# Where the modulation columns of a hybrid decoder layer are computed, and four output tiles written one by one

## The chip, the cores and the metric

The kernel runs on one core of one Trainium2 chip, in one launch. The metric is the device time of an execution in microseconds (us); the median of three runs stands for a kernel. About 0.2% is what a measurement of this kernel can tell from no change.

## The reference

One layer on x of 256 rows and 2048 columns, in f32, with three residual parts, each behind an RMSNorm that is shifted, scaled and gated by vectors computed from a conditioning row c:

```python
cond = jax.nn.silu(c)
mod = cond @ ada_w[l] + ada_b[l]                       # 9 vectors of 2048
sh1, sc1, gt1, sh2, sc2, gt2, sh3, sc3, gt3 = jnp.split(mod, N_MOD, axis=-1)
h = ada_in(x, norm_g[l, 0], sh1, sc1)                  # rmsnorm(x)*g*(1+sc) + sh
x = x + MACARON_W * gt1[:, None, :] * swiglu(h, ...)   # SwiGLU_1, inner width 5632
h = ada_in(x, norm_g[l, 1], sh2, sc2)
x = x + gt2[:, None, :] * hybrid_mixer(h, w_in[l], w_out[l], ...)   # 8 heads forgetting attention, 8 heads gated delta net
h = ada_in(x, norm_g[l, 2], sh3, sc3)
x = x + MACARON_W * gt3[:, None, :] * swiglu(h, ...)   # SwiGLU_2
...
return rmsnorm(x, final_norm)
```

## The kernel before, in words

**Layout.** x is held transposed: 16 tiles `x[:, j]` of 128 features by 256 rows. All weights are cut into 5392 tiles of 128 by 128 and laid out in DRAM in the order in which TensorE uses them, eight to a block, so there are 674 blocks of 512 KB. `Stream.next` hands out the next tile. At the first tile of a block it loads the block (`wraw`, on SP's queue), ScalarE rounds it to the high half `whi` (L127), and VectorE subtracts to get the low half `wlo` (L139). A product of f32 precision is made of three matmul terms: high by high, high weight by low activation, low weight by high activation. Raw, high and low halves have four buffers each, so a block's halves can be made up to three blocks ahead of TensorE.

**Stages by blocks.** SwiGLU_1 is done in two parts of its inner width. Blocks 0 to 111 are the gate and up products of its first 28 inner tiles (`gate_up_first`, matmuls L572 to L574 into `pgu`), 112 to 167 their down products, 168 to 263 the second part. The mixer's input projections are blocks 264 to 377, with the chains of the heads woven in; its output projection is blocks 378 to 409 (`po`, L492 and L493, two matmuls a tile). SwiGLU_2 takes the rest.

**The first stage** cannot have all of its input h at once, since h needs the modulation columns sc1 and sh1. The list `PIECES` cuts the contraction into pieces (group of eight inner tiles, first k, k from which a tile is finished on its own, end k). At the end of a piece the partial sums are moved out of PSUM: first copied by ScalarE, then added on VectorE (`acc`, L587), and with the last piece two adds (L590, L591), SiLU, a product (L523) and a split in halves (L506, L507) make the tile `hid`.

**The modulation columns.** The 9 vectors are 144 columns of 128 values. A column is one 1 MB load of 128 rows of `ada_w` (`adat`, on SP's queue) and one multiply-and-add-up on VectorE (L264) into `mod`. Two are made before the stream begins. The others are side work of the stream: at each block the rate of that block in `RATE` is added to a counter, and each time it reaches 1, `ada_col` issues the next column. The order is sc1 and sh1 by turns, then gt1, sh2, sc2, gt2, sh3, sc3, gt3. `ada_need` computes at once whatever is missing when a column is wanted; with both tables of rates every column has been issued by then. Inside the mixer (`W.late`) the VectorE part is put off by two blocks.

**Order of work.** The engines' programs are written out in program order by a scheduler that lets a later instruction go ahead only where the earlier one isn't ready in its own estimate of time; on the chip each engine then runs its list in that fixed order.

**The output projection.** The first four output tiles j = 0 to 3 are accumulated together in four PSUM banks, 64 weight tiles or 8 blocks, because the last head isn't ready at the start. Tiles 4 to 15 follow one by one, 16 weight tiles or 2 blocks each. The epilogue `after` of a tile does the gated residual (`residual`, L516 and L517), the square for the next norm (ScalarE, then GpSimd adds), and `norm2.y`, which scales the tile by 1 + sc3 for SwiGLU_2 (g at L389, high half on ScalarE L415, low half on VectorE L416). The epilogues of tiles 0 to 3 stand right behind the last of their products; the epilogue of each later tile stands in the next tile's products at i = `LATER` = 8 of 16.

Of the kernel before, what the change touches and what calls it, by code (L numbers as in the profile page):

```python
# [19 lines left out]
KD = D // P  # L20
# [12 lines left out]
GR = 24  # L33
NEG = -1e30

RATE = ((0, 0.5), (12, 0.45), (68, 0.06), (112, 0.5), (168, 0.38), (264, 0.0), (284, 0.26), (404, 0.0), (424, 0.125))
N_BIG, N_GDN = 3, 3
N_FIRST = 2
AHEAD = 4
# [2 lines left out]
HIDX = 3  # L42
MORE = True
LATER = 8
BEHIND = 2

HA = 128 + 16
# [45 lines left out]
class Stream:  # L93
# [36 lines left out]
    def next(self, mat, k, n, width=1):  # L130
        i = len(self.order)
        if i % WB == 0:
# [3 lines left out]
            self.l = lo.tile([P, WB * P], F32R, name="wlo")  # L136
            pace = [r_ for r_ in RATE if r_[0] <= b][-1][1]
            with self.behind():
                lo_ = nc.vector.tensor_tensor(self.l, r, self.h.bitcast(F32), ALU.subtract)  # L139
            with self.tc.issue_after(lo_.ins):  # L140
                self.settle(b - BEHIND)
            self.owed += 0.0 if self.quiet else pace
# [11 lines left out]
def layer_kernel(ctx: ExitStack, tc: tile.TileContext, xrow, c, adaw, cols, cst, w, out, order, dbg=None):  # L154
# [14 lines left out]
    def psb(name="psb"):  # L169
        return big.tile([P, 512], F32, name=name, tag="psb")  # L170

    def pss(name="pss"):
        return sml.tile([P, 512], F32, name=name, tag="pss")

    def psf(name="psf"):
        return sm2.tile([P, 512], F32, name=name, tag="psf")

    def psn(i, name):

        i %= 8  # L180
        return psb(name) if i < N_BIG else pss(name) if i < N_BIG + N_GDN else psf(name)
# [5 lines left out]
    x = keep.tile([P, KD, T], F32, name="x")  # L187
# [85 lines left out]
    def ada_need(m, j):  # L273

        while ada_st["i"] < ada_seq.index((m, j)) + 1:
            ada_col()
        W.settle()
# [23 lines left out]
    def sqrt_table(after):  # L301

        d = tiny.tile([P, 1], F32, name="dummy")
        return A.activation(d, after, AF.Sqrt, scale=0.0)

    def sumsq_add(j):

        if j == 0:
            sqa["acc"] = tmp.tile([P, T], F32, name="sqacc", bufs=1)
            A.activation(sqa["acc"], x[:, j], AF.Square)  # L310
            return
        s = tmp.tile([P, T], F32, name="sq")
        A.activation(s, x[:, j], AF.Square)
        if j == KD - 1:
            sqa["src"] = [sqa["acc"], s]
        else:
            G.tensor_tensor(sqa["acc"], sqa["acc"], s, ALU.add)
# [152 lines left out]
    def tick(us):  # L470
        clock["now"] += us
        for kind in chains:
            if chains[kind] and clock["now"] >= due[kind]:
                advance(kind)

    def finish(kind, h):

        while chains[kind] and chains[kind][0][0] <= h:
            advance(kind)
# [11 lines left out]
    def mm(ps, wt, act, first, last):  # L491
        PE.matmul(ps, wt[0], act.rearrange("p q (a b) -> p q b a", a=2), start=first, stop=False)  # L492
        PE.matmul(ps[:, :T], wt[1], woven(act[:, 0]), start=False, stop=last)  # L493
# [15 lines left out]
    def residual(ps, j, m_gt, half):  # L509
        ada_need(m_gt, j)  # L510
        g = mod[:, m_gt * KD + j : m_gt * KD + j + 1]
        if half:
            gh = tiny.tile([P, 1], F32, name="gh")
            V.tensor_scalar(gh, g, 0.5, None, ALU.mult)
            g = gh
        V.scalar_tensor_tensor(x[:, j], ps[:, :T], g, x[:, j], ALU.mult, ALU.add)  # L516
        i = V.scalar_tensor_tensor(x[:, j], ps[:, T:], g, x[:, j], ALU.mult, ALU.add)  # L517
        sqa["hold"] = i.ins
# [109 lines left out]
    def ffn(which, m_gt, early=None):  # L628
        fs = list(range(NF))
        with tc.tile_pool(name=f"hid{which}", bufs=PARTS[which][1] + HIDX) as hp, \  # L630
                tc.tile_pool(name=f"more{which}", bufs=1) as more:
            W.more = more if MORE else None
            for half in range(2):
# [7 lines left out]
                def after(j):  # L641
                    residual(pds.pop(j), j, m_gt, True)
                    if half == 1:
                        sumsq_add(j)
                        if which == 1:
                            if j < KD - 1:
                                A.activation(x[:, j], x[:, j], AF.Copy, scale=L("fng", j, 1))
                            else:
                                V.tensor_scalar(x[:, j], x[:, j], L("fng", j, 1), None, ALU.mult)
                        if j == KD - 4:  # L650
                            W.quiet = True
                        if j == KD // 2:
                            sqrt_table(x[:, j, :1])

                for j in range(KD):
                    ps = psb("pd")
                    for q, hd in enumerate(hids):
                        if j and q == LATER:
                            after(j - 1)
# [19 lines left out]
    for kind, i in (("x", 0), ("x", 1), ("c", 0), ("c", 1), ("x", 2), ("x", 3), ("c", 2), ("c", 3)):  # L679
        with nullcontext() if hold is None else tc.issue_after(hold):  # L680
            if kind == "c":
                hold = cond(i)
            else:
                t, q = divmod(i, 2)
# [64 lines left out]
    norm2 = Early(2, 6, 7)  # L749
# [5 lines left out]
    def mixer():  # L755
# [23 lines left out]
        def x_back(q):  # L779
            with tc.issue_after(W.last):  # L780
                nc.sync.dma_start(x[:, 4 * q : 4 * q + 4], xd[:, 4 * q : 4 * q + 4])
# [499 lines left out]
        owed = []  # L1281
        ko = [NH + h for h in range(4)] + list(range(6)) + [NH + h for h in range(4, NH)] + [6, 7]
        for js in [list(range(4))] + [[j] for j in range(4, KD)]:

            j = js[0]
            one_ = psf if j < 6 or j >= KD - 2 else pss if j < 8 else psb
            pj = [psn(i, "po") for i in range(len(js))] if len(js) > 1 else [one_("po")]
            if js[0] in BACK:
                x_back(1 + BACK.index(js[0]))
            for i, k in enumerate(ko):  # L1290
                for kind in ("gdn", "out") if k >= NH else ("fox",):
                    finish(kind, k % NH)
                if js[0] == 0 and i == KD - 1:
                    x_back(0)
                if owed and i == LATER:
                    owed.pop(0)()
                for q, j in enumerate(js):
                    mm(pj[q], W.next("o", k, j), oh_[k], i == 0, i == KD - 1)
                    tick(TILE_US)

            def after(js=js, pj=pj):
                for q, j in enumerate(js):
                    residual(pj[q], j, 5, False)
                    sumsq_add(j)
                    norm2.y(j)
                    if j == KD // 2:
                        sqrt_table(x[:, j, :1])

            if j == 3 or j == KD - 1:
                after()  # L1310
            else:
                owed.append(after)
        mx.close()

    if dbg is None or "mix" in dbg:
        mixer()
# [154 lines left out]
```

## Time and profile before

| | before |
|---|---|
| median of 3 runs | 1944.64 us (1944.19 to 1946.02) |
| profiled execution, its own time | 1944.91 us |
| its span, first to last instruction | 1943.1 us |
| TensorE (PE) matmul busy | 1903.0 us, 98% |
| VectorE (DVE) busy | 1555.1 us, 80% |
| ScalarE (ACT) busy | 1039.5 us, 53% |
| mean granted clock of TensorE | 0.993 |
| modulation columns on VectorE | 142, 334.6 us |
| low halves on VectorE | 674, 820.8 us |

The profile is one execution. A line of the timeline gives the start in us, the duration, the engine, the source line, the operation, its output and inputs, and in square brackets the idle time of the engine ahead of it and what ended that. A line of a list of waits gives who waited for whom, the total in us, how many times and the longest. A line of windows gives busy time and number of instructions of each engine in that stretch, the clock granted to TensorE (1.00 is full), and the share and rate of the DMA engines. A line of groups gives number, busy time and mean duration in ns. Busy times of successive instructions overlap a little, because an instruction starts before the one ahead has drained.

### The profile page before, as it was taken

Reading aid. Unit: us, or ns where it says so; the run is one execution under the profiler, and the core shown is the slowest. Engines: PE = TensorE matmul, PEld = TensorE weight load, DVE = VectorE, ACT = ScalarE, POOL = GpSimd, SP = SyncE. Lnnn points to the kernel's source line nnn. Section 1 sums busy time; section 2 is a strip of 40 time slices with the busy share of each in tenths; the row PEclk is TensorE's granted clock in tenths of the full one; section 3 lists DMA queues with packets and bytes.
Section 4 is the critical chain, followed back from the end, with each engine's and each line's share of the span. In section 5 each row is a group of like instructions: output and inputs, shape, how many; then the busy total and the mean of one; then the engine's idle time right before and its main releaser. Section 6 shows DMA issues by size and latency. Waiting matters only on the chain.

```text
span 1943.1 us, 33703 instructions
## 1 busy us (share of the span) xinstructions
PE 1903.0 (98%) x13086; PEld 1774.5 (91%) x13087; DVE 1555.1 (80%) x2414; ACT 1039.5 (53%) x1647; POOL 57.4 (3%) x55
## 2 busy tenths in 40 slices
PE   8999999999999999999999999999999999999998
PEld 7999999988999988889989998999999999999997
DVE  6999888989999997789987989877676765666654
ACT  7433555433455446857757655665554445555553
POOL 0000000000000020000000002100000000000011
PEclk9999999999999999999999999999999999999999
DMA  9998867999989985596567567677777766666663
GB/s 374 350 344 345 294 215 265 400 374 376 361 347 348 349 307 211 197 330 219 204 254 250 207 229 281 206 246 264 240 246 262 244 231 199 203 199 202 200 201 120
DMA packets 129490, 519.58 MB, mean 267 GB/s; under 512 B 18217, under 2 KB 21545, under 8 KB 111153
## 3 DMA queue, kind: packets, MB, share of 16 engines
q1 hardware_dynamic: 129330, 517.42, 74.1%
q8 instruction: 103, 1.69, 0.3%
q14 instruction: 57, 0.47, 0.1%
HBM read 512.89 MB, written 4.47 MB: 266 GB/s over the span
## 4 chain that ended last, share of the span: by engine, by line
PE 77%; DVE 12%; issue 4%; ACT 3%; DMA 2%; SPq 0%; DVEq 0%; ACTq 0%
PE pd L492 12%; PE pu L488 10%; PE pg L488 10%; PE pd L493 6%; PE pu L489 5%; PE pg L489 5%; DVE wlo L139 5%; PE pgu L574 4%; PE pgu L572 4%; PE pgu L573 4%; DVE adat L264 3%; PE po L492 2%; PE pp L795 2%; PE pp L796 2%; PE pp L797 2%
## 5 line engine op out<-in xcount | busy, mean ns | idle before, releaser
L139 DVE TENSOR_TENSOR wlo<-wraw,whi 128x1024 fp32r<-128x1024 f32 x674 | 820.8, 1225 | 263.8 <-ACT whi L127 262.6
L127 ACT CAST whi<-wraw 128x1024 fp32r<-128x1024 f32 x674 | 698.3, 1045 | 509.4 <-PE pd L492 178.1
L492 PE MATMUL pd<-hid,whi 128*128 128x512 f32 x1408 | 462.1, 382 | 0.0
L493 PE MATMUL pd<-hid,wlo 128*128 128x256 f32 x1408 | 384.8, 274 | 2.7 <-DVE wlo L139 2.7
L264 DVE CUSTOM_DVE_ANT_0 adat<-adat,cs,colt 128x2048 f32<-128x2048 f32 x142 | 334.6, 2357 | 7.6 <-DMA adat<-in_ada_dram 7.4
L488 PE MATMUL pg<-hs,whi 128*128 128x512 f32 x912 | 302.1, 382 | 0.5 <-DVE shc L439 0.5
L488 PE MATMUL pu<-hs,whi 128*128 128x512 f32 x912 | 302.2, 382 | 0.0
L492 PEld LDWEIGHTS pd<-hid,whi 128*128 128x128 f32 x1408 | 266.0, 189 | 36.7 <-DVE hid L507 0.2
L493 PEld LDWEIGHTS pd<-hid,wlo 128*128 128x128 f32 x1408 | 270.2, 192 | 6.0 <-DVE wlo L139 5.6
L489 PE MATMUL pu<-hs,wlo 128*128 128x256 f32 x912 | 249.3, 273 | 0.0
L574 PE MATMUL pgu<-hs,wlo 128*128 128x256 f32 x896 | 240.7, 278 | 8.3 <-DVE wlo L139 8.0
L489 PE MATMUL pg<-hs,wlo 128*128 128x256 f32 x912 | 248.8, 273 | 0.0
L572 PE MATMUL pgu<-hs,whi 128*128 128x256 f32 x896 | 244.8, 276 | 0.8 <-DVE acc L587 0.5
L573 PE MATMUL pgu<-hs,whi 128*128 128x256 f32 x896 | 244.5, 276 | 0.0
L488 PEld LDWEIGHTS pg<-hs,whi 128*128 128x128 f32 x912 | 172.4, 189 | 24.9 <-ACT shc L438 0.7
L488 PEld LDWEIGHTS pu<-hs,whi 128*128 128x128 f32 x912 | 172.4, 189 | 23.6
L795 PE MATMUL pp<-hs,whi 128*128 128x256 f32 x656 | 188.4, 288 | 1.1 <-ACT hs L379 1.1
L797 PE MATMUL pp<-hs,wlo 128*128 128x256 f32 x656 | 182.2, 278 | 0.0
L796 PE MATMUL pp<-hs,whi 128*128 128x256 f32 x656 | 181.9, 277 | 0.0
L574 PEld LDWEIGHTS pgu<-hs,wlo 128*128 128x128 f32 x896 | 168.8, 193 | 11.0 <-DVE wlo L139 10.8
L489 PEld LDWEIGHTS pu<-hs,wlo 128*128 128x128 f32 x912 | 175.0, 192 | 1.4 <-DVE wlo L139 1.4
L489 PEld LDWEIGHTS pg<-hs,wlo 128*128 128x128 f32 x912 | 175.1, 192 | 0.3
(335 smaller groups left out, 2585.9 us busy)
## 6 DMA issues: line engine op xcount, KB each, us to landing
wraw<-in_w_dram SPq DMA_DIRECT2D x674, 512.0 KB, 4.4
adat<-in_ada_dram SPq DMA_DIRECT2D x142, 1024.0 KB, 7.5
xr<-in_xr_dram SPq DMA_DIRECT2D x4, 512.0 KB, 5.6
adaf<-in_ada_dram SPq DMA_DIRECT2D x4, 512.0 KB, 8.5
xd<-x SPq DMA_DIRECT2D x4, 512.0 KB, 6.9
rw<-rowd SPq DMA_DIRECT2D x16, 128.0 KB, 4.2
x<-xd SPq DMA_DIRECT2D x4, 512.0 KB, 5.6
out_dram<-o SPq DMA_DIRECT2D x8, 256.0 KB, 2.6
```

The costliest lines, as they stand in the source:

```text
L127: self.cast = self.nc.scalar.copy(self.h, r).ins
L139: lo_ = nc.vector.tensor_tensor(self.l, r, self.h.bitcast(F32), ALU.subtract)
L264: V.tensor_tensor_reduce(t, t, cs, 1.0, L("adab", q, 1), ALU.mult, ALU.add, mod[:, q : q + 1])
L488: PE.matmul(ps, wt[0], both, start=(k == 0), stop=False)
L489: PE.matmul(ps[:, T:], wt[1], part(k, HI), start=False, stop=(k == KD - 1))
L492: PE.matmul(ps, wt[0], act.rearrange("p q (a b) -> p q b a", a=2), start=first, stop=False)
L493: PE.matmul(ps[:, :T], wt[1], woven(act[:, 0]), start=False, stop=last)
L572: PE.matmul(o, wh, part(k, HI), start=first and s == 0, stop=False, skip_group_check=skip)
L573: PE.matmul(o, wh, part(k, LO), start=False, stop=False, skip_group_check=skip)
L574: PE.matmul(o, wl, part(k, HI), start=False, stop=last, skip_group_check=skip)
L795: PE.matmul(pp[i][:, :T], wh, hh, start=(k == 0), stop=False)
L797: PE.matmul(pp[i][:, :T], wl, hh, start=False, stop=(k == KD - 1))
```

## The change

Three things change. The table of rates gets new stretches in SwiGLU_1: blocks 28 to 32 and 49 to 55 have a rate of 0.25, the others up to 65 have 0.5, and blocks 66 to 111 have 0.2 instead of 0.45 and 0.06. The mixer's input projections have 0.255 up to block 375, and from there to 423 the rate is 0, which takes in the output projection; from 424 it is 0.16. The epilogues of the first four output tiles no longer stand together behind their products: each goes on the list `owed`, as those of the later tiles do, and as long as that list has more than one, two of them are taken per output tile, at i = 3 and i = 11; else one at i = 8. Whatever is left is done at the end.

```diff
-RATE = ((0, 0.5), (12, 0.45), (68, 0.06), (112, 0.5), (168, 0.38), (264, 0.0), (284, 0.26), (404, 0.0), (424, 0.125))
+RATE = ((0, 0.5), (28, 0.25), (33, 0.5), (49, 0.25), (56, 0.5), (66, 0.2), (112, 0.5), (168, 0.38), (264, 0.0), (284, 0.255), (376, 0.0), (424, 0.16))
...
 LATER = 8
+SLOTS = (3, 11)
...
             one_ = psf if j < 6 or j >= KD - 2 else pss if j < 8 else psb
+            slots = SLOTS if len(owed) > 1 else (LATER,)
...
-                if owed and i == LATER:
+                if owed and i in slots:
                     owed.pop(0)()
...
-            def after(js=js, pj=pj):
-                for q, j in enumerate(js):
-                    residual(pj[q], j, 5, False)
-                    sumsq_add(j)
-                    norm2.y(j)
-                    if j == KD // 2:
-                        sqrt_table(x[:, j, :1])
-
-            if j == 3 or j == KD - 1:
-                after()
-            else:
-                owed.append(after)
+            def after(j, ps):
+                residual(ps, j, 5, False)
+                sumsq_add(j)
+                norm2.y(j)
+                if j == KD // 2:
+                    sqrt_table(x[:, j, :1])
+
+            owed += [lambda j=j, ps=ps: after(j, ps) for j, ps in zip(js, pj)]
+        while owed:
+            owed.pop(0)()
         mx.close()
```

## The prediction

> **What bounds the kernel now.** I read the page first, then the list of waits of TensorE, then the windows of 5 us around each wait, then VectorE's timeline inside those windows. The share of busy time of TensorE leaves 40 us of the span.
>
> ```profile
> span 1943.1 us, 33703 instructions
> PE 1903.0 (98%) x13086; PEld 1774.5 (91%) x13087; DVE 1555.1 (80%) x2414; ACT 1039.5 (53%) x1647; POOL 57.4 (3%) x55
> ```
>
> So a gain has to come out of single waits of TensorE, or out of stretches in which its clock was low. The waits that this change can reach are these; wlo is the low half of a block of eight weight tiles, which VectorE makes by one subtraction, in program order with everything else that it does.
>
> ```profile
> PE pgu L574 <- DVE wlo L139: 8.0, 10, 2.3
> PE po L493 <- DVE wlo L139: 2.0, 1, 2.0
> PE po L492 <- ACT whi L127: 0.7, 1, 0.7
> PE pgu L572 <- DVE acc L587: 0.5, 2, 0.3
> ```
>
> pgu is the first gate/up stage of SwiGLU_1, po the output projection. TensorE's steady rate there is read from two undisturbed windows (PE, PEld, DVE, ACT, POOL busy with counts, then clock, DMA share, GB/s): 450 matmuls at 3 a tile in 50 us are 2.67 us for a block of 8 tiles; 1223 at 2 a tile in 200 us are 2.62 us.
>
> ```profile
> 250.00:300.00 50.00, 50.00 (x450) 50.00 (x450) 38.35 (x56) 25.45 (x36) 0.00 (x0) 1.00 0.72 234
> 1300.00:1500.00 200.00, 200.00 (x1223) 183.69 (x1222) 142.13 (x175) 99.72 (x143) 0.00 (x0) 1.00 0.74 251
> ```
>
> **The output projection.** It runs from block 378 to 409. The windows that hold wlo alone count the blocks (busy us of VectorE, number, clock, DMA share, GB/s):
>
> ```profile
> 0.00:1168.10 1168.10, 470.98 (x389) 0.99 0.80 298
> ...
> 0.00:166.90 166.90, 60.00 (x50) 0.99 0.92 355
> ```
>
> Blocks count from 0, so the subtraction at 1168.02 belongs to block 388 and the next one, at 1178.32, to block 389; in the same way 166.98 is block 50. Between them VectorE does the epilogues of the first four output tiles in one go, and one modulation column (adat):
>
> ```profile
> 1168.02 1.23 DVE L139 TENSOR_TENSOR wlo<-wraw,whi 128x1024 fp32r<-128x1024 f32 x1 [2.70 <-ACT whi L127]
> 1169.17 0.87 DVE L516 SCALAR_TENSOR_TENSOR x<-po,mod,x 128x256 f32<-128x256 f32 x2
> ...
> 1173.80 2.40 DVE L264 CUSTOM_DVE_ANT_0 adat<-adat,cs,colt 128x2048 f32<-128x2048 f32 x1
> ...
> 1178.32 1.21 DVE L139 TENSOR_TENSOR wlo<-wraw,whi 128x1024 fp32r<-128x1024 f32 x1
> ```
>
> ```profile
> 1175.81 0.60 PE L492 MATMUL po<-oh,whi 128*128 128x512 f32 x2
> ```
>
> TensorE runs out of low halves at about 1176.1 and waits, and the two slices from 1175 us show the rest of the bill: 11 and 22 matmuls where an undisturbed slice of 5 us has 33 (before it), and a clock of 0.68 after the wait.
>
> ```profile
> 1165.00:1170.00 5.00, 5.00 (x33) 4.64 (x32) 2.30 (x5) 1.48 (x2) 0.00 (x0) 1.00 1.01 390
> ...
> 1175.00:1180.00 5.00, 2.30 (x11) 1.53 (x11) 5.00 (x9) 2.04 (x3) 2.58 (x2) 0.98 0.01 4
> 1180.00:1185.00 5.00, 5.00 (x22) 4.39 (x22) 5.00 (x7) 1.89 (x3) 1.06 (x1) 0.68 0.89 340
> ```
>
> 33 matmuls short are 5.0 us. The waits alone are 2.7, and the clock costs 5 x 0.32 + 5 x 0.02 = 1.7, together 4.4. I take the middle, 4.7 us, as the price of this place.
>
> What the change does here. The epilogues now stand in the order at slots 3 and 11 of the following tiles, so only three of them (slot 3 and 11 of tile 4, slot 3 of tile 5) come before wlo 389, and no column. Prices of VectorE's work in this stage:
>
> ```profile
> L139 DVE TENSOR_TENSOR wlo<-wraw,whi 128x1024 fp32r<-128x1024 f32 x31 | 38.2, 1236 | 5.0 <-ACT whi L127 5.0
> L264 DVE CUSTOM_DVE_ANT_0 adat<-adat,cs,colt 128x2048 f32<-128x2048 f32 x7 | 16.5, 2350 | 0.0
> L416 DVE SCALAR_TENSOR_TENSOR hs<-x,g,hs 128x256 fp32r<-128x256 f32 x15 | 13.5, 904 | 0.2 <-ACT hs L415 0.2
> L517 DVE SCALAR_TENSOR_TENSOR x<-po,mod,x 128x256 f32<-128x256 f32 x15 | 7.1, 486 | 0.1
> L516 DVE SCALAR_TENSOR_TENSOR x<-po,mod,x 128x256 f32<-128x256 f32 x15 | 7.0, 476 | 0.0
> L389 DVE SCALAR_TENSOR_TENSOR g<-mod,colt 128x1 f32<-128x1 f32 (+1 forms) x15 | 2.3, 160 | 0.1
> ```
>
> By durations an epilogue is 0.476 + 0.486 + 0.904 + 0.160 = 2.03 us. Successive instructions overlap a little: from 1169.17 to 1178.32 are 9.15 us, less one column of 2.35 leaves 6.8 for four epilogues, 1.70 each. Three of them end at 1169.17 + 5.1 = 1174.3, wlo 389 is done at 1175.5, and TensorE needs it when block 388 ends, about 1176.1. The wait goes. What is late next is the run of tiles 4 to 6, each with two epilogues: 2 x 1.70 + 2 x 1.13 = 5.67 us of VectorE against 2 x 2.62 = 5.23 of TensorE, three times 0.44 = 1.3 us, of which the margin at block 389 pays 0.6. That is a stall of up to 0.7; if epilogues don't overlap (2.03 and 1.24), three times 1.3 less 0.6 is 3.3. I take 0.5, because the 1.70 was measured in this place. So the projection gains 4.7 - 0.5 = 4.2 us, bounds 1.4 and 5.0. The other six columns that leave lie beside a TensorE that doesn't wait; taking 2.35 us each from a free VectorE earns nothing. ScalarE's two operations per tile only move with their tile. On SP's queue seven loads of a column go with them:
>
> ```profile
> adat<-in_ada_dram SPq DMA_DIRECT2D x142, 1024.0 KB, 7.5
> ```
>
> No weight block that TensorE waits for here was held up by one (its wait was for wlo, and the DMA stood at 0.01 during it), so their leaving earns nothing, and they join stages counted below.
>
> **The columns of SwiGLU_1.** A running sum of the rates gives the block at which each column is issued. Up to block 27 there are 13 before and 14 after; in 28 to 32 two against one; in 33 to 48 seven against eight; in 49 to 55 three against two; at block 65 both have 30. From 66 to 111 three become nine. The waits lie where eight partial sums are added in a burst (acc), with a column in it:
>
> ```profile
> 72.64 0.38 PE L574 MATMUL pgu<-hs,wlo 128*128 128x256 f32 x1 [0.58 <-DVE wlo L139]
> ...
> 105.62 0.38 PE L574 MATMUL pgu<-hs,wlo 128*128 128x256 f32 x1 [2.25 <-DVE wlo L139]
> 119.04 0.38 PE L574 MATMUL pgu<-hs,wlo 128*128 128x256 f32 x1 [0.43 <-DVE wlo L139]
> ...
> 168.25 0.38 PE L574 MATMUL pgu<-hs,wlo 128*128 128x256 f32 x1 [2.25 <-DVE wlo L139]
> ```
>
> Counted by wlo, these are blocks 17, 28, 33 and 50. With the waits for acc the first place costs 0.58 + 0.5 = 1.1.
>
> Block 50. Before, VectorE idles 2.19 us ahead of the burst and then has a column inside it:
>
> ```profile
> 157.31 0.69 DVE L587 TENSOR_TENSOR acc<-pgu,acc 128x512 f32<-128x512 f32 x1 [2.19 <-PE pgu L574]
> ...
> 162.91 2.34 DVE L264 CUSTOM_DVE_ANT_0 adat<-adat,cs,colt 128x2048 f32<-128x2048 f32 x1
> ```
>
> After, the columns are those of blocks 48 and 51: the first fits the idle 2.19, the second comes behind wlo 50. That makes wlo 50 2.34 us earlier against a wait of 2.25: gain 2.25, nothing if column 48 is put into the burst. Behind this wait the clock also fell, worth 5 x 0.05 + 5 x 0.29 = 1.7; behind the equal wait at 105.62 it did not:
>
> ```profile
> 105.00:110.00 5.00, 4.38 (x39) 4.38 (x40) 5.00 (x6) 1.05 (x1) 0.00 (x0) 1.00 0.71 222
> ...
> 165.00:170.00 5.00, 2.75 (x22) 2.55 (x22) 5.00 (x8) 1.05 (x1) 0.00 (x0) 0.95 0.80 293
> 170.00:175.00 5.00, 5.00 (x34) 5.00 (x33) 5.00 (x7) 1.67 (x3) 0.00 (x0) 0.71 0.85 291
> ```
>
> Block 33. One column fewer lies between blocks 28 and 33: gain 0.43, against nothing if the loss at block 28 carries on to here.
>
> Blocks 17 and 18. Columns of 14, 16, 18 become 13, 15, 17, so one more lies before the burst and still one inside it ahead of wlo 18, and it stands nearer to it.
>
> ```profile
> 65.60 1.29 DVE L587 TENSOR_TENSOR acc<-pgu,acc 128x512 f32<-128x512 f32 x2 [0.61 <-PE pgu L574]
> ...
> 74.30 1.22 DVE L139 TENSOR_TENSOR wlo<-wraw,whi 128x1024 fp32r<-128x1024 f32 x1
> ...
> 94.62 0.69 DVE L587 TENSOR_TENSOR acc<-pgu,acc 128x512 f32<-128x512 f32 x1 [0.55 <-PE pgu L574]
> ```
>
> One column (2.35), less the idle 0.61 that VectorE had before the burst, makes wlo 18 1.7 us later, done at 75.5 + 1.7 = 77.2; TensorE got wlo 17 at 72.6, so it wants wlo 18 one block later, at 75.3, and 0.7 earlier if the waits ahead of 17 shrink: 1.9 to 2.6. Bounds 0.5 (only the waits for acc) and 2.6 + 0.5, against 1.1 before; I take 2.2: loss 1.1.
>
> Block 28. The column of 27 stays in the burst, and one more lies ahead: 2.35, less the 1.1 that TensorE has lost meanwhile and the 0.55 idle of the last row, 0.7 later. Bounds 0 and 1.8 (that loss left out); I take 0.8, so the wait is about 3.1 us. The clock fell after one of the two equal waits of 2.25; I put one fall of 1.7 behind this longer one. [...]
>
> Blocks 66 to 111. Six more columns, 14 us, fall where VectorE has room at first (38.35 of 50) and little at the end:
>
> ```profile
> 285.00:337.00 52.00, 52.00 (x463) 51.87 (x462) 45.90 (x78) 30.08 (x48) 0.00 (x0) 1.00 0.71 247
> ```
>
> ```profile
> L507 DVE TENSOR_TENSOR hid<-tu,hid 128x256 fp32r<-128x256 f32 x14 | 5.9, 421 | 1.2 <-ACT hid L506 1.2
> ...
> L590 DVE TENSOR_TENSOR tg<-pgu,acc 128x256 f32<-128x256 f32 x13 | 5.4, 417 | 0.2 <-PE pgu L574 0.2
> ```
>
> Two or three more columns make 50.6 to 53.0 of 52 here. The three blocks that VectorE is ahead (8 us) cover it; I put 0.4, bounds 0 and 6.4 (a rival, below). These loads raise a DMA share of 0.72.
>
> Sum for SwiGLU_1: -2.25 - 0.43 + 1.1 + 0.8 + 0.4 and two clock falls that cancel, -0.4 us.
>
> **Elsewhere.** From 424 on 15 columns instead of 13 lie under a TensorE that was busy 200 of 200 us with VectorE at 142: nothing, or 4.7 if that cover were gone. The mixer's projections keep 24 columns at other blocks: 0, with 1 us either way.
>
> The profiled execution took 1944.91 us, 0.27 over the median: 1944.91 - 4.2 - 0.4 = 1940.3, so 1940.0 as a median. About 0.2% (3.9 us) can be told from no change; this is 0.24%.
>
> **The rivals.** No clock fall in SwiGLU_1: the wait at 28 leaves the clock at 1.00 as at 105.62, 1.7 less, 1938.3. [...] Against it stands the row of 0.71. Chance 0.17.
>
> The epilogue wait comes back: two epilogues per tile without overlap, 3.3 instead of 0.5 at blocks 391 to 392, 1942.8. For it speaks that an epilogue goes through ScalarE between its VectorE steps; against it the 1.70. Chance 0.18.
>
> Slower: VectorE gets to block 98 without its lead. There four operations per feature tile, two adds, a product and a subtraction (0.42 each by the two rows of that window; a tile takes 1.25 blocks, then 1) join wlo and 0.2 columns: 1.22 + 1.34 + 0.47 = 3.03 and then 3.37 us against 2.67, ten blocks x 0.36 + four x 0.70 = 6.4, with two clock falls 9.8, instead of 0.4: 1949.4. It decides when the lead at 98 is under two blocks; overlapped starts, which make the sums nearly even, and the 6.1 us that VectorE idles in the window from 285 speak against it. Chance 0.12.
>
> The projection's wait stays: it was the order of ScalarE's high halves (0.7 of the wait) and not VectorE's queue; 1944.2. Chance 0.06.
>
> **How the numbers follow.** The forecast has 0.47, with 0.03 of it above 1940.75. Faster: 0.44 + 0.17 = 0.61; same: 0.03 + 0.18 + 0.06 = 0.27; slower 0.12. The likeliest alone spans 1938.5 to 1941. The range, 1935.8 to 1945.0, goes down by the 1.1 and 0.8 not lost, the rival's 1.7 and most of the 0.8 between 4.2 and 5.0, and up over all but the slower case.
>
> **What would show it.** Right: no po wait for wlo above 0.7 and clock 1.00 around 1180; the pgu wait at block 50 gone; waits near 2 and 3 us at blocks 18 and 28. Wrong: a pgu wait beyond 300 us, pairs of po waits near block 391, or a wait at block 50 still there.

## The result and the profile after

| | before | after |
|---|---|---|
| median | 1944.70 us (1941.33 to 1947.07) | 1949.32 us (1944.96 to 1955.54) |
| ratio | | 1.0025, 95% interval 1.0019 to 1.0032 |
| profiled execution, its own time | 1944.91 us | 1948.17 us |
| span | 1943.1 us | 1946.4 us |

One disturbed run of after, 1983.32 us, is left out of its range and of the ratio; without it the median of after is 1948.62. The change made the kernel slower by 0.25%; the forecast was 1940.0. The page of after and the first lines of its list of waits of TensorE (total, times, longest; line numbers are one higher than before):

```profile
span 1946.4 us, 33719 instructions
PE 1900.8 (98%) x13086; PEld 1773.9 (91%) x13087; DVE 1558.7 (80%) x2414; ACT 1040.3 (53%) x1645; POOL 56.8 (3%) x55
```

```profile
PE pgu L575 <- DVE wlo L140: 14.3, 12, 2.8
PE pd L494 <- DVE wlo L140: 4.8, 10, 1.5
```

The waits of the output projection (po) for low halves are no longer on the list, as forecast. In exchange the waits of pgu, the first gate/up stage, went from 8.0 to 14.3, and those of pd, the down products, from 2.7 to 4.8.

A wait shows where TensorE stood, but not all of what a stage lost. The first and last start of a stage's matmuls give that. These are such rows of a tile's instructions (the times are those of the first and the last start): pgu and po of before, then pgu, pd and po of after.

```profile
L572 PE MATMUL pgu<-hs,whi x896: 275/275/460, 19.2 to 334.9; 128*128 128x256 f32 x180
L492 PE MATMUL po<-oh,whi x256: 379/382/631, 1141.2 to 1235.4; 128*128 128x512 f32 x128
```

```profile
L573 PE MATMUL pgu<-hs,whi x896: 275/275/460, 18.8 to 341.9; 128*128 128x256 f32 x180
L493 PE MATMUL pd<-hid,whi x704: 379/382/382, 342.2 to 749.2; 128*128 128x512 f32 x176
L493 PE MATMUL po<-oh,whi x256: 382/382/567, 1151.1 to 1238.7; 128*128 128x512 f32 x128
```

The last pd of SwiGLU_1 stood at 740.0 before, so the span divides into stages:

| us | before | after | |
|---|---|---|---|
| to the first pgu | 19.2 | 18.8 | -0.4 |
| pgu, blocks 0 to 111 | 315.7 | 323.1 | **+7.4** |
| rest of SwiGLU_1 | 405.1 | 407.3 | +2.2 |
| mixer up to the projection | 401.2 | 401.9 | +0.7 |
| output projection | 94.2 | 87.6 | **-6.6** |
| from there to the end | 707.7 | 707.7 | 0.0 |

The sum is +3.3, the difference of the spans. Within the stage pgu the first product of block 66 starts at 212.0 us before and at 209.2 after: blocks 0 to 65 became 2.4 us shorter, and blocks 66 to 111 went from 122.9 to 132.7, 9.8 longer. The loss sits in two windows that had TensorE busy 50.00 of 50 us before (busy us of PE, PEld, DVE, ACT, POOL, then clock, DMA share, GB/s):

```profile
250.00:300.00 50.00, 46.64 (x413) 46.26 (x412) 36.35 (x49) 21.36 (x30) 0.00 (x0) 0.99 0.67 239
300.00:350.00 50.00, 44.72 (x366) 43.59 (x366) 42.90 (x75) 27.18 (x44) 0.00 (x0) 0.97 0.73 267
...
295.00:300.00 5.00, 2.93 (x24) 2.74 (x23) 5.00 (x7) 1.16 (x3) 0.00 (x0) 0.94 0.18 70
300.00:305.00 5.00, 5.00 (x34) 5.00 (x34) 4.49 (x9) 2.94 (x5) 0.00 (x0) 0.72 0.80 253
```

That is 8.6 us of waiting (7.1 of it in pgu, 1.5 at the first down products), and a clock of 0.94 and 0.72 around one of the waits, which ended at 298.94 after TensorE had stood 2.07. VectorE was not full: 36.35 of 50 us in the first window, fewer than the 38.35 of before, with more columns to do. It stood. What it waited for is in its own waits between 205 and 350 us, of before and of after:

```profile
DVE adat L264 <- DMA adat<-in_ada_dram: 2.6, 1, 2.6
```

```profile
DVE adat L265 <- DMA adat<-in_ada_dram: 17.4, 6, 3.9
```

So VectorE came to a modulation column before the column's 1 MB load had landed, six times, and stood there with the low halves queued behind it. One turn of this in the timelines of VectorE and of the load queue (SP) of after:

```profile
278.99 2.35 DVE L265 CUSTOM_DVE_ANT_0 adat<-adat,cs,colt 128x2048 f32<-128x2048 f32 x1 [3.87 <-DMA adat<-in_ada_dram]
...
281.94 1.22 DVE L140 TENSOR_TENSOR wlo<-wraw,whi 128x1024 fp32r<-128x1024 f32 x1
...
283.40 1.22 DVE L140 TENSOR_TENSOR wlo<-wraw,whi 128x1024 fp32r<-128x1024 f32 x1
...
284.94 1.23 DVE L140 TENSOR_TENSOR wlo<-wraw,whi 128x1024 fp32r<-128x1024 f32 x1
...
294.73 2.35 DVE L265 CUSTOM_DVE_ANT_0 adat<-adat,cs,colt 128x2048 f32<-128x2048 f32 x1 [3.76 <-DMA adat<-in_ada_dram]
```

```profile
283.18 0.33 SPq L125 DMA_DIRECT2D wraw<-in_w_dram  x1
...
284.69 0.33 SPq L125 DMA_DIRECT2D wraw<-in_w_dram  x1
...
286.19 0.33 SPq L125 DMA_DIRECT2D wraw<-in_w_dram  x1
286.57 0.43 SPq L261 DMA_DIRECT2D adat<-in_ada_dram  x1
```

Each load of a weight block starts when a low half is done (281.94 + 1.22 = 283.16, and 283.18), because that frees a raw buffer. (In SwiGLU_1 there is a fifth raw buffer besides the four, so the low half of a block frees the buffer of the block five later.) The column's load stands in SP's queue behind the third of them. It is issued 7.58 us after the column before it began, and the next column can start 8.16 us later. The loop is closed: column, three low halves, raw buffer, weight block, column load, column, 15.74 us for five blocks that TensorE would do in 13.35 (5 x 2.67). VectorE stood 17.4 us in all and TensorE only 8.6, so about 8.8 us were paid from the three blocks that VectorE is ahead; then TensorE waits too. In VectorE's fixed order the last five columns of this stage stand behind the low half of block b-3, where b is the block behind whose load the column's own load is issued; up to block 65 a column stands right behind the low half of b itself.

### The profile page after: what moved, and what is told of

The parts are those of the page before. It is cut to its first block, busy times and chain, and to the rows that moved or that the text cites. A ratio compares the mean times of both kernels' runs of the same rounds, so it can differ in the third digit from the quotient of the medians.

```text
span 1946.4 us, 33719 instructions
## 1 busy us (share of the span) xinstructions
PE 1900.8 (98%) x13086; PEld 1773.9 (91%) x13087; DVE 1558.7 (80%) x2414; ACT 1040.3 (53%) x1645; POOL 56.8 (3%) x55
## 4 chain that ended last, share of the span: by engine, by line
PE 75%; DVE 11%; DMA 5%; issue 5%; ACT 3%; SPq 0%; DVEq 0%; ACTq 0%
PE pd L493 14%; PE pg L489 10%; PE pu L489 10%; PE pd L494 7%; PE pu L490 5%; PE pg L490 5%; DVE wlo L140 4%; PE po L493 3%; DMA adat<-in_ada_dram 2%; PE pgu L575 2%; PE pgu L573 2%; PE pgu L574 2%; PE pp L796 2%; PE pp L797 2%; PE pp L798 2%
## 5 line engine op out<-in xcount | busy, mean ns | idle before, releaser
L575 PE MATMUL pgu<-hs,wlo 128*128 128x256 f32 x896 | 240.6, 278 | 14.7 <-DVE wlo L140 14.3
```

The costliest lines, as they stand in the source:

```text
L575: PE.matmul(o, wl, part(k, HI), start=False, stop=last, skip_group_check=skip)
```

## The experiments

Each heading names the kernel, before or after, that the edit starts from. Times are medians; the kernel before, run beside them, had 1944.96 in the first four, 1945.55 in the next four, 1945.58 in the last four. Stage times and waits are those of one profiled execution each.

**After, with the VectorE part of the columns put off in blocks 66 to 111, by the switch alone**:

```diff
+            if b in (66, 112):
+                self.late = b == 66
```

> The changed kernel, with the VectorE part of each column issued in blocks 66 to 111 put off by two blocks (as the mixer does it already); loads, number of columns and all work are the same. Theory 'landing': VectorE stands still for 17 us in that stage because a column stands in its fixed order ahead of the landing of its load, and the low halves stand behind it; then the waits of VectorE for adat between 205 and 350 us fall from 17.4 us to under 3, the waits of TensorE there from 8.6 us to under 1.5, and the time from 1949.3 to 1937 to 1941 us. Theory 'work' (six more columns overload VectorE) and theory 'traffic' (six more 1 MB loads delay the weight blocks): both are unchanged here, so 1947 to 1951 us.

1950.46 us, ratio to before 1.0025 (1.0015 to 1.0035); waits of VectorE for columns in the stage 18.0 us. The edit moved nothing: `ada_need` is called at every tile of this stage and settles what is owed at once, so VectorE's columns stand behind the same low halves as in after. It tells nothing between the theories and stands as a second measurement of the change.

**Before, with the epilogues of the first four output tiles one by one** (that part of the diff, the old table of rates):

> The epilogue part alone: the kernel before with its own table of rates, but the epilogues of output tiles 0 to 3 one by one. Seven columns stay in the output projection. If the pile of epilogues was the cause of the wait at block 389 (my step): the po wait of 2.7 us and the clock fall behind it go, 1940 to 1942 us. If the column there was needed too, a wait of 1 to 3 us stays around blocks 389 to 392, 1942 to 1945 us.

1945.25 us, ratio 0.9997 (0.9989 to 1.0006). The projection took 93.4 us instead of 94.2; waits for low halves of 1.3 us stayed instead of 2.7, and the clock stayed at 1.00, which bears out part of the step. But the columns were still there, and one of them stood elsewhere in the new order: computed at 1160.72, ahead of the last head's `on`, it came with a new wait of TensorE:

```profile
PE pft L1216 <- DVE on L1212: 2.0, 1, 2.0
```

Taken together the epilogues alone are worth nothing that can be measured.

**Before, with the new rates up to block 65 only**:

```diff
-RATE = ((0, 0.5), (12, 0.45), (68, 0.06), ... (424, 0.125))
+RATE = ((0, 0.5), (28, 0.25), (33, 0.5), (49, 0.25), (56, 0.5), (66, 0.06), ... (424, 0.14))
```

> The new rates of blocks 0 to 65 alone, 0.06 as before from 66 to 111, the rest of the kernel before (0.14 instead of 0.125 from block 424, so that no column is missing at the end). By the traces: head 2 us better in waits and no clock fall behind block 50, so 1940.5 to 1943 us. If the fall of the clock comes anywhere in this stage all the same, 1942.5 to 1945.

1944.22 us, ratio 0.9992 (0.9984 to 1.0001); the first stage took 315.0 us instead of 315.7. That is the second expectation: this profile has a clock fall behind block 28 (0.75 in the slice from 105). The head of the stage does not carry the loss.

**Before, with rate 0.2 in blocks 66 to 111**:

```diff
-(12, 0.45), (68, 0.06), (112, 0.5)
+(12, 0.45), (66, 0.2), (112, 0.5)
```

> The new rate of 0.2 in blocks 66 to 111 alone, in the kernel before (0.45 from block 12 to 65 kept). Theories 'landing', 'work' and 'traffic' all say that the loss sits here: 8.6 us of waits and one to two clock falls, 1953 to 1957 us, with waits of VectorE for adat of 14 to 20 us. If the loss came from another part of the change, 1943 to 1946 us.

1946.23 us, ratio 1.0004 (0.9995 to 1.0012). This is far below both the 1953 to 1957 expected and the changed kernel: as many columns as after (nine), but VectorE waited for them only 6.8 us, at most 2.0, and TensorE 1.8; the first stage took 316.5. The columns fell on blocks 69, 74, ... instead of 70, 75, .... In this kernel the columns of the projection moved too, none into the burst of epilogues, and with the burst and seven columns still there the projection took 89.0, with 0.7 of waits for low halves and no clock fall.

**After, with these columns one block earlier, and three blocks earlier** (69, 74, ... and 67, 72, ...):

```diff
-(66, 0.2), (112, 0.5)
+(66, 0.4), (67, 0.2), (111, 0.0), (112, 0.5)
```

```diff
-(66, 0.2), (112, 0.5)
+(66, 0.8), (67, 0.2), (109, 0.0), (112, 0.5)
```

> The changed kernel with the nine columns of blocks 66 to 111 one block earlier each: 69, 74, ... instead of 70, 75, ...; as many columns, as much work, the same distance of three blocks between a load and its place in VectorE's order. Theory 'place in the cycle' (raw buffers go round in five blocks, so a column every fifth block always meets the same buffer): the wait of VectorE for a column between 205 and 350 us falls from 17.4 to 7 us or less, TensorE's waits there from 8.6 to 3 or less, and the time is 1940 to 1944. Theory 'standing ahead' (a column three blocks ahead of its load's landing makes VectorE stand, wherever the load is): waits as in the changed kernel, 1948 to 1950.5. Theory 'work' (VectorE is full there): the same 1948 to 1950.5, but with VectorE's waits gone.

> The same columns three blocks earlier: 67, 72, ... 107. Theory 'place in the cycle': a third place gives a third cost, somewhere between 1940 and 1949.5, and other waits than in the run with one block. Theories 'standing ahead' and 'work': 1948 to 1950.5, as the changed kernel.

One block: 1945.74 us, ratio 1.0002 (0.9994 to 1.0011). Three blocks: 1943.61 us, 0.9994 (0.9985 to 1.0003). VectorE stood 10.4 and 10.9 us, TensorE 3.5 in both, and the stage took 315.8 and 316.3. Neither time lies in the 1948 to 1950.5 of 'standing ahead' and 'work'; that of one block is above the 1940 to 1944 of 'place in the cycle' too, that of three blocks is in its range. So the block at which a column falls counts, with the work the same. One turn of the kernel with one block (SP, then VectorE):

```profile
280.92 0.33 SPq L125 DMA_DIRECT2D wraw<-in_w_dram  x1
...
282.05 0.33 SPq L125 DMA_DIRECT2D wraw<-in_w_dram  x1
...
285.09 0.33 SPq L125 DMA_DIRECT2D wraw<-in_w_dram  x1
285.47 0.42 SPq L261 DMA_DIRECT2D adat<-in_ada_dram  x1
```

```profile
277.39 2.35 DVE L265 CUSTOM_DVE_ANT_0 adat<-adat,cs,colt 128x2048 f32<-128x2048 f32 x1 [2.11 <-DMA adat<-in_ada_dram]
...
291.05 2.35 DVE L265 CUSTOM_DVE_ANT_0 adat<-adat,cs,colt 128x2048 f32<-128x2048 f32 x1 [1.46 <-DMA adat<-in_ada_dram]
```

The three weight blocks ahead of the column's load are spread over 4.2 us instead of 3.0, because the adds of an inner tile fall between the second and the third low half, and the load lands 5.6 us after its issue instead of 8.2. The loop is 13.66 us, near the 13.35 of TensorE. That the bunching makes the landing longer is read from these turns; no run changed the bunching alone. With three blocks the longest of the middle turns was longer than that of after (268.39 to 284.50 is 16.1 us), but VectorE stood only 0.3 at the first of its five waits and 0.5 at the last, and some columns stand nearer to the low half of their block there. In both runs about 7 us of VectorE's standing did not reach TensorE, near the 8.8 of after.

**After, with the VectorE part really put off by two blocks** in 66 to 111, so that it stands behind the low half of block b+2 instead of b-3:

```diff
+            if b in (66, 112):
+                self.late = b == 66
...
-                ada_need(0, k)
+                if not W.late:
+                    ada_need(0, k)
```

> The changed kernel with the VectorE part of the columns of blocks 66 to 111 put off by two blocks, so that it stands five blocks later in the fixed order (behind the low half of block b+2 instead of b-3); loads where they were. Theory 'standing ahead': VectorE's waits for a column between 205 and 350 us go from 17.4 to under 1, TensorE's there from 8.6 to 0 to 2, the clock stays at 1.00, and the time is 1938 to 1942, what the prediction had. Theory 'work': 1947 to 1950.5, since VectorE has the same work. Theory 'place in the cycle': the loads take as long as before but nobody waits, so the same 1938 to 1942; the two runs with shifted columns tell it from 'standing ahead'.

1942.70 us, ratio 0.9988 (0.9980 to 0.9997), just above the 1938 to 1942 expected. The loads are the same, so is the work on VectorE, and its waits are gone (waits of this kernel between 205 and 350 us, and two windows at the end of the stage):

```profile
PE pd L496 <- DVE wlo L142: 2.3, 1, 2.3
...
DVE adat L267 <- DMA adat<-in_ada_dram: 0.4, 1, 0.4
```

```profile
335.00:340.00 5.00, 2.67 (x16) 2.14 (x15) 5.00 (x10) 2.59 (x5) 0.00 (x0) 0.94 0.74 292
340.00:345.00 5.00, 5.00 (x24) 4.41 (x24) 5.00 (x5) 1.04 (x1) 0.00 (x0) 0.72 0.83 292
```

The first stage took 314.8 us, 8.3 less than after, with one clock fall in both. So neither VectorE's work nor the traffic of the six more loads made the loss of this stage; the place of the column in the order did. What is left is one wait of 2.3 us as the down products begin, with a clock of 0.72 behind it, after the adds of the last tiles and two columns 6.4 us apart (327.89 and 334.31): VectorE is full there (5.00 of 5). The rest of SwiGLU_1 took 409.9.

**After, with 0.06 in blocks 66 to 111 as before**, the columns that are missing there in the mixer's input projections instead:

```diff
-(66, 0.2), (112, 0.5), (168, 0.38), (264, 0.0), (284, 0.255)
+(66, 0.06), (112, 0.5), (168, 0.38), (264, 0.0), (284, 0.335)
```

> The changed kernel with the rate of the kernel before (0.06) from block 66 to 111: three columns there instead of nine, and the six that are missing made in the mixer's input projections (0.335 instead of 0.255). If the whole loss lies in blocks 66 to 111 and the gain of the output projection is real: 1938.5 to 1942. If the rest of the change earns nothing by itself: 1943.5 to 1946. If the loss lies elsewhere: 1947 or more. The six columns in the mixer may cost up to 1 us.

**1939.44 us, ratio 0.9969 (0.9959 to 0.9979).** All of the rest of the change is worth 6 us. By the sum of the rates, and by the trace, two columns are left in blocks 66 to 111 here and not three, and the mixer's projections have 31 instead of 24. The first stage took 316.0, the output projection 87.6, and the mixer 400.0: the seven more columns there cost nothing in this execution.

**After, with a column in every sixth block** of 66 to 111:

```diff
-(66, 0.2), (112, 0.5), ... (284, 0.255)
+(66, 0.1667), (112, 0.5), ... (284, 0.285)
```

> The changed kernel with a column in every sixth block (71, 77, ... 107) instead of every fifth of blocks 66 to 111, seven instead of nine; the two others in the mixer (0.285 instead of 0.255). Theory 'closed loop' (column, three low halves, a free raw buffer, the load of a weight block, the load of the next column behind it, 8.2 us of landing: 15.75 us by the trace of the changed kernel, against 5 x 2.67 = 13.35 that TensorE allows): TensorE now allows 6 x 2.67 = 16.0 us, so VectorE goes on standing 2 to 4 us at a column, but TensorE's waits between 205 and 350 us go from 8.6 to 0 to 2, and the time is 1938.5 to 1942. Theory 'work' (VectorE has too much to do): seven ninths of the loss stay, 1945 to 1949.

1944.21 us, ratio 0.9994 (0.9986 to 1.0002): between the two expectations.

```profile
DVE adat L265 <- DMA adat<-in_ada_dram: 12.3, 6, 3.5
...
PE pgu L575 <- DVE wlo L140: 2.7, 2, 1.9
```

VectorE went on standing, as the loop wants, and TensorE waited 2.7 instead of 8.6. The 15.74 was the wrong figure to compare with 16.0: with six blocks there are four low halves from the column to the next load, and the turns took 16.2 to 17.4 us (from the starts of the columns at 261.51, 278.89, 295.06, 312.24 and 329.45). Each turn is about 1 us too long, against 2.4 with five. This profile also had a clock fall at 336 us and two in the mixer, which took 404.7.

**Before, with its four epilogues in one go, and the whole table of the kernel with 0.06** (no column in the projection):

> The kernel before, with its four epilogues in one go, and the table of rates of the run with 0.06 in blocks 66 to 111 (1939.4): no column in the output projection. Theory 'the column made the wait' (four epilogues and a column were 9.15 us, without the column 6.8): TensorE's wait for wlo in the projection falls from 2.7 to 0.2 to 0.8, the clock stays at 1.00, 1939 to 1941.5. Theory 'the burst made it': a wait of 2 or more and a low clock behind it, 1942.5 to 1944.5.

1939.71 us, ratio 0.9971 (0.9962 to 0.9981). Without a wait for low halves the projection is as short as after:

```profile
L492 PE MATMUL po<-oh,whi x256: 382/382/567, 1141.6 to 1229.2; 128*128 128x512 f32 x128
```

So the burst alone makes no wait, and with the columns gone the epilogues one by one add nothing (87.6 us both). This run took all seven columns out; that it is the one in the burst that counts most is seen in the run with 0.2 alone, 89.0 with seven columns in other places.

**The kernel with 0.06 and the column of block 27 put at 29, and the same with the three columns of blocks 66 to 111 put off** (the columns of 31 and 51 move by one block too, and the sum of the rates now leaves three columns in blocks 66 to 111):

```diff
-(0, 0.5), (28, 0.25), (33, 0.5), (49, 0.25), (56, 0.5)
+(0, 0.5), (26, 0.25), (32, 0.5), (49, 0.25), (54, 0.5)
```

> The run with 0.06 in blocks 66 to 111, and beside it the column of block 27 put at 29, behind the burst of adds (32, 52 instead of 31, 51; the rest as there). If that column makes the wait of 2.8 us at block 28: the wait falls to 0.3 to 1.0, no clock fall there, 1935 to 1938 (2.0 less for the wait, up to 1.7 more where the clock had fallen). If the adds alone make it: 1938.5 to 1941.

> The same as the run with the column of block 27 at 29, and the VectorE part of the three columns of blocks 66 to 111 put off by two blocks. Those three columns kept VectorE waiting 4.0 us and TensorE 0.9 us in the run with 0.06: up to 1 us less than the run beside it, or nothing if VectorE's lead covers it.

The first: **1934.31 us, ratio 0.9942 (0.9929 to 0.9955)**, the lowest median of all and just under the 1935 to 1938 expected. The second: 1936.34 us, 0.9952 (0.9940 to 0.9964), no gain from putting off; a wait of 0.9 us appeared in the down products. The place at block 28 with the column at 27 and at 29:

```profile
105.00:110.00 5.00, 2.28 (x18) 2.09 (x17) 5.00 (x10) 1.88 (x3) 0.00 (x0) 0.95 0.29 112
110.00:115.00 5.00, 5.00 (x34) 5.00 (x34) 4.98 (x5) 1.04 (x1) 0.00 (x0) 0.70 0.83 255
```

```profile
105.00:110.00 5.00, 5.00 (x45) 4.83 (x44) 5.00 (x6) 2.09 (x2) 0.00 (x0) 1.00 1.02 388
110.00:115.00 5.00, 5.00 (x47) 5.00 (x47) 5.00 (x9) 2.95 (x4) 0.00 (x0) 1.00 0.98 391
```

Wait and clock fall are gone; the first stage took 311.8.

## Why the prediction was wrong, by its own steps

**The step that failed is "Blocks 66 to 111".** The prediction put 0.4 there. It added up VectorE's work, found room at first, and let "the three blocks that VectorE is ahead (8 us)" cover the rest. Measured: these blocks took 9.8 us longer, of which 7.1 are waits of TensorE for low halves and 1.7 a clock fall (5 x 0.06 + 5 x 0.28), with 1.0 unaccounted for; the rest of SwiGLU_1 took 2.2 longer, with 4.8 instead of 2.7 of waits in the down products. A column was taken as 2.35 us of work. It also is a wait for its load, and that load stands behind the weight blocks whose buffers VectorE itself must free. The waits of VectorE before held a sign, the 2.6 us at a column in the same stage (quoted above). The forecast never asked for these waits, only for what TensorE waited for, and took three columns becoming nine as work alone.

**The slower rival had the time and mostly not the cause.** It said 1949.4, by VectorE's work in blocks 98 to 111. Its 6.4 and two clock falls add up to the 9.8 measured, by chance: the put-off columns do the same work with a first stage of 314.8 us, so work is not what it cost. It is right for a remainder: at the end of the stage VectorE is full, and the wait of 2.3 us with its clock fall makes most of the 5.4 us by which the rest of SwiGLU_1 is longer in the put-off kernel than in the one with 0.06 (409.9 against 404.5).

**The output projection: right in sign, too small, and for the wrong half of the edit.** 4.2 was forecast with bounds 1.4 and 5.0; the stage became 6.6 shorter. The 4.7 of cost was the mean of 4.4 and 5.0, from slices that end at 1185, and 0.5 went off for a stall that did not come (no wait for low halves in the whole stage). Another 1.6 lies ahead of the burst, where the prediction put nothing: in the first 30 us of the stage TensorE starts 75 weight tiles before and 80 after, 5 x 0.33 us. Its cause stays open: the columns computed there (one at 1155.28) can't be all of it, since the run with 0.2 alone has three columns in the same stretch and starts 80 too. The prediction credited both the missing column and the moved epilogues; the run with the burst and no column shows that taking the columns out is enough. The sum was there to see: four epilogues without the column, 6.8 us, are 2.35 shorter than the 9.15 that caused a wait of 2.7. (The 6.8 also holds the first add of a fifth epilogue, at 1177.86, so 1.70 for one is a little high.) One of the text's premises was off as well: one column is still computed in this stage, near its end (at 1228.08, with 1.22 us of VectorE standing). No columns are issued in the last blocks of SwiGLU_1, which the count of columns had missed (it had 15 from block 424 on; the trace has 16), so this one was still missing when its tile wanted it and `ada_need` issued it on the spot. TensorE did not wait there.

**SwiGLU_1 up to block 65: near, and the clock by luck.** Without the 0.4 of blocks 66 to 111 the sum was 0.8 shorter; it became 2.4 shorter in this profile, and 0.9 and 0.8 in those of the first and the third experiment, which have this head with a clock fall in it. Block 33: its wait is gone (0.43). Block 50: 1.00 us of TensorE idle in 160 to 175 instead of 2.44, and no clock fall; the forecast had 2.25 gained. Blocks 17 and 18: waits of 0.76 and 0.65 instead of 2.2 forecast. Block 28: 2.8 us of idle instead of 2.5, where 3.1 was forecast, from these slices of after:

```profile
100.00:105.00 5.00, 3.81 (x32) 3.42 (x30) 5.00 (x8) 1.64 (x3) 0.00 (x0) 1.00 0.79 319
105.00:110.00 5.00, 3.38 (x30) 3.39 (x31) 5.00 (x6) 2.22 (x3) 0.00 (x0) 1.00 0.42 116
```

Of the clock fall put there, this profile has none. But six of the nine profiles of kernels with this head have one at this place, and three have none. The length of the idle time does not part them: it is 2.8 us from 100 to 110 us in after (clock 1.00), in the kernel with 0.06 (0.70 in the slice behind, quoted above) and in the kernel with a column in every sixth block (0.88 over these 10 us).

In the traces of before and after, each fall inside the program is a stretch at a clock of 0.50 that lasts 3.41 us or twice that, and the falls of one trace start at whole multiples of 3.413 us from each other (after: 9.26, 299.40, 753.37 and 818.22 us, which are 85, 133 and 19 multiples). By these numbers a fall of 3.41 us is worth an estimated 1.7 us; the slices of the kernel with 0.06 above give 1.75 (5 x 0.05 + 5 x 0.30). With this grid laid over block 28, the same idle time falls apart in one trace and not in another. Here are after, and then the first experiment, whose matmuls stand in the same order and whose wait at this place is the same 2.72 us:

```profile
101.43:104.84 3.41, 2.46 (x23) 2.27 (x21) 3.41 (x7) 0.55 (x2) 0.00 (x0) 1.00 0.70 281
104.84:108.25 3.41, 1.64 (x14) 1.64 (x15) 3.41 (x5) 1.33 (x2) 0.00 (x0) 1.00 0.22 53
```

```profile
105.88:109.29 3.41, 0.69 (x6) 0.50 (x5) 3.41 (x7) 1.88 (x3) 0.00 (x0) 1.00 0.09 32
109.29:112.70 3.41, 3.41 (x19) 3.41 (x17) 3.41 (x4) 0.61 (x1) 0.00 (x0) 0.50 0.70 205
```

In the first experiment all 2.72 us lie in the one stretch just ahead of its fall; in after the grid cuts them in two, 0.95 and 1.77. It is the same with the two equal waits of the profile before: 2.17 us in one stretch at block 50, with a fall, and 1.27 and 0.98 at block 28, without. That is what these four places show and no more: in before a fall at 742.93 comes behind a stretch with 1.47 us of idle time, and in after none comes behind the 1.86 us in the stretch from 12.68. So the prediction's choice of one fall at block 28 and one fewer at block 50 could not be had from the length of the waits. The grid lies elsewhere in the two traces above (edges at 104.84 and 109.29), and a fall that is worth 1.7 us came in one and not in the other; the profile of after has none at block 28 and was that much luckier than six of these nine.

**Elsewhere.** From block 424 on nothing changed (707.7 us both). The mixer was forecast as 0 with 1 either way: +0.7 after; over all runs it lay between 399.1 and 404.7, at 399 to 401 in the five profiles with a clock of 1.00 from 800 to 900 us and at 401 to 405 in the nine with one or two falls there (0.93 or 0.97 in a slice of 50 us). All fourteen also lose about 3 us to a lower clock between 700 and 800 us (in before and after 6.83 us at 0.50, at the start of the mixer). The chain of small steps there was not followed up.

## What to carry to other kernels

When work with its own load is moved in a fixed order, count from the issue of the load to the instruction that needs it, and ask what must happen before the load can be issued: here the waiting engine itself freed the buffers, so every turn of the loop came out longer than TensorE's (15.7 to 16.8 us in after, against 13.35), however idle the engine looked. Read the waits of the engine ahead of the bound, not only those of the bound; a single stand of 2.6 us in the profile before was the warning. And where a burst stalls the bound by about the length of one movable item in it, move that item alone: the columns taken out of the projection (6.6 us) and the one moved at block 28 (4.2 us of the first stage, with its clock fall) made most of the 0.6% of the fastest kernel here, and the larger edit of the epilogues was not needed.

## What was not expected of the hardware

The 1 MB load of a column landed 5.6 us after its issue with three weight blocks issued in the 4.6 us before it, and 8.2 us with three in the 3.4 us before it. Idle time of TensorE of equal length (2.72 us at block 28) was followed by a clock of 0.50 for 3.41 us in the first experiment, where all of it lay in one stretch of the 3.41 us grid, and by none in after, where at most 1.77 did. And the first gate product started at 18.8 to 19.2 us in eight profiles and at 20.9 to 21.3 in six, whatever the kernel. That is a spread of 2 us in comparing single profiles; its cause stays open.
